# A new opening for a one-core encoder layer: products of ones while x lands, x in four transfers, a first power ahead of time, h by two engines, and two z heads ended before the other two

## The chip, the cores and the metric

The kernel runs on one core of one Trainium2 chip. Its engines work side by side, each in the order of its own queue: TensorE (PE, with its weight loads shown as PEld), VectorE (DVE), ScalarE (ACT), GpSimd (POOL) and SyncE (SP), which here issues every transfer between HBM and the on-chip memory. The metric is the device time of one execution in microseconds (us).

## The reference

One layer of a hybrid encoder runs over two sequences: a prompt of 2048 tokens and a sample of 32 tokens with a carried state. The width is 1024, everything is float32. What matters here:

```
cs = silu(c);  mod = cs @ ada_w + ada_b            # 6 x 1024 columns: shift, scale, gate, twice
h  = rmsnorm(x, norm_mix_g) * (1 + sc1) + sh1
p  = h @ w_in                                       # u, v | q, k, v | z | a, b
a_out = u * (W_s rmsnorm(v) + b_s)                  # spatial gating, 128-token chunks
q, k, v = silu(causal_conv(qkv));  q, k = l2norm(q), l2norm(k)
o  = gated_delta_rule(q, k, v, beta, g, state)      # 4 heads x 128, in chunks
b_out = rmsnorm(o) * silu(z)                        # z: 4 heads x 128 columns of p
x  = x + gt1 * (concat(a_out, b_out) @ w_out)
x  = x + gt2 * (relu((rmsnorm(x) * (1 + sc2) + sh2) @ w_up)^2 @ w_down)
y  = rmsnorm(x, final_norm_g)
```

The mean of squares in `rmsnorm` is taken over the 1024 features of a token. The features lie on the partitions (8 tiles of 128, counted by k), so that mean is a sum over partitions and tiles.

## The kernel before

The tokens are worked on in two halves (hf 0: tokens 0 to 1023, hf 1: the rest and the sample), and each half in groups of up to 512. Every large product is made three times with rounded operands: a matrix is split into a high part and the rest (`wh`, `wl` for weights, `BH`, `BL` for h; numbered 0 to 7 by k), and wh*BH, wh*BL and wl*BH are added up in PSUM. The splitting is one copy on ACT (the high part) and one subtraction on DVE (the rest). Weights come as slabs of 256 columns; a slab is loaded in two transfers, the first half of it for k 0 to 3, the second for k 4 to 7. Two slabs fit on the chip, so that the next one is split only when the last product of the one before it in the same place is done.

PSUM has eight banks, named by their use: g0, g1, g2 and L3 for the large products, C4 and C5, B6, M7. On-chip places are "slots" (s0 to s27). Most helpers record an operation: `act`, `tt` (two tensors), `ts` (tensor with scalars), `dma`, `mms` (products), `tr` (transpose on PE). All operations of one helper have one line in the profile: L339 for ACT, L354 for `tt`, L368 for `ts`, L377 for a DVE copy, L392 for the transfers, L400 for products, L411 for transposes.

The order is not that of the text. `Program.schedule` puts all recorded operations in an order by estimated costs and latencies, by a priority for each (the large products are behind everything else) and by the order in which they were recorded; each engine then runs its share of that order strictly. A change at the start thus moves work on every engine until the plan has settled again.

The opening, `startup`, does this for the first 512 tokens: load x (eight transfers of 128x512), square it on ACT, add the squares on DVE into `row`, then `rms_row`: four products with a column of ones (M7) give the sums per token, DVE scales them, POOL raises them to the power -0.5 (`rcol`), four transposes spread them over 128 partitions (M7), and ACT copies that to `row`. In parallel `ada_first(f, ps)` makes shift and scale for tile f: two transfers of 128x1024 (`ada0`, a ring of four places), two groups of four narrow products (C4 or C5; 2x256), an ACT copy, two transposes back, four small additions on DVE (`modc`) and one `ts` (the column `a1`). `h_tile` then multiplies x by `row` (DVE, for k 2 and 5 POOL), scales and shifts it (DVE, POOL or ACT by k) and splits it into `BH` and `BL`. For each k all four z heads get their three products (`gemm_k`; banks g0, g1, g2, L3; slab 0 serves heads 0 and 1, slab 1 heads 2 and 3). Then follow the second 512 tokens in the same manner, and `v_stage`, whose products (128x260) read h as the weights of PE. The mixers, the output projection and the feed-forward part come after that, unchanged in their code.

## Time and profile before

| | us |
|---|---|
| median of 3 runs | 2353.92 |
| lowest, highest | 2351.38, 2355.38 |
| the profiled execution, its own time | 2350.23 |
| its span, from the first to the last instruction | 2348.5 |
| PE busy | 2299.2 |
| DVE busy | 1678.7 |
| ACT busy | 1226.9 |
| POOL busy | 598.8 |

The profiled execution is 3.69 us shorter than the median and 1.7 us longer than its span. PE is busy for 98% of the span. In a row of the timeline stand the start, the busy time, the engine, the line, the operation, what it writes and reads, the shape and the count, and in brackets how long the engine had been idle and what ended that. PE counts each product of plain float32 operands twice in the profile (four products are x8), those of the split operands once.

### The profile page before, as it was taken

How to read it: one execution, taken by the hardware profiler on the slowest of the kernel's cores; microseconds unless marked ns; L12 is line 12 of the kernel's file. 1: busy time of each engine (PE TensorE's matmuls, PEld its weight loads, DVE VectorE, ACT ScalarE, POOL GpSimd, SP SyncE). 2: the span in 40 equal slices, each digit the busy share in tenths (PEclk: the TensorE clock that was granted, in tenths of full speed). 3: DMA queues.
4: the chain of work that ended last, by engine and by line, in shares of the span. 5: the costliest groups of instructions: out<-in, count | busy, mean ns of one | idle time of the engine just before them, and what ended most of it. 6: DMA issues, size and time to landing. Idle time of an engine off the chain costs nothing. (4 is left out here: it accounts for less than half of the span.)

```text
span 2348.5 us, 45724 instructions
## 1 busy us (share of the span) xinstructions
PE 2299.2 (98%) x15882; PEld 2171.3 (92%) x15882; DVE 1678.7 (71%) x3675; ACT 1226.9 (52%) x2817; POOL 598.8 (25%) x827
## 2 busy tenths in 40 slices
PE   7999999999999999999999999999999999999998
PEld 4877878999999888999999989999999999999998
DVE  6556557666665656589999999877667786666775
ACT  4465657455565535376555646664433564334343
POOL 2235421312432322445444434210000050000001
PEclk9999999999999999999999999999999999999999
DMA  9698668465557778888777787998667797666771
GB/s 321 225 333 280 199 189 258 141 187 178 151 175 228 241 220 251 256 269 270 243 252 259 258 269 248 335 323 266 211 219 250 251 294 247 214 220 219 238 232 53
DMA packets 369263, 556.27 MB, mean 237 GB/s; under 512 B 71212, under 2 KB 191424, under 8 KB 369032
## 3 DMA queue, kind: packets, MB, share of 16 engines
q1 hardware_dynamic: 369032, 553.35, 72.8%
q8 instruction: 125, 2.05, 0.4%
q14 instruction: 106, 0.87, 0.1%
HBM read 398.92 MB, written 154.28 MB: 236 GB/s over the span
## 5 line engine op out<-in xcount | busy, mean ns | idle before, releaser
L339 ACT ACTIVATE s<-s 128x348 fp32r<-128x348 f32 (+13 forms) x1079 | 494.9, 482 | 365.3 <-DVE s L354 145.5
L400 PE MATMUL f<-s,wh 128*128 128x348 f32 (+1 forms) x2760 | 662.0, 322 | 6.7 <-DVE s L359 5.4
L400 PEld LDWEIGHTS f<-s,wh 128*128 128x128 f32 x2760 | 480.2, 189 | 10.2 <-DVE s L359 6.2
L354 DVE TENSOR_TENSOR s<-f,s 128x348 f32<-128x348 f32 (+1 forms) x696 | 348.9, 514 | 175.3 <-PE f L400 174.2
L400 PE MATMUL f<-s,wl 128*128 128x348 f32 (+1 forms) x1380 | 444.1, 322 | 0.3 <-DVE wl L354 0.3
L400 PE MATMUL g<-BH,wh 128*128 128x512 f32 (+2 forms) x1112 | 421.8, 379 | 0.7 <-DVE s L359 0.7
L400 PE MATMUL g<-BH,wl 128*128 128x512 f32 (+2 forms) x1112 | 391.7, 352 | 0.0
L354 DVE TENSOR_TENSOR s<-s,s 128x348 fp32r<-128x348 f32 (+9 forms) x688 | 356.4, 547 | 49.2 <-ACT s L339 21.2
L400 PE MATMUL g<-BL,wh 128*128 128x512 f32 (+2 forms) x1112 | 390.6, 351 | 0.0
L400 PE MATMUL f<-BL,wh 128*128 128x348 f32 (+1 forms) x1016 | 329.0, 324 | 4.9 <-DVE BL L354 4.9
L400 PE MATMUL f<-BH,wl 128*128 128x348 f32 (+1 forms) x1016 | 328.1, 323 | 1.1 <-DVE wl L354 1.1
L400 PE MATMUL f<-BH,wh 128*128 128x348 f32 (+1 forms) x1016 | 328.4, 323 | 0.0
L339 ACT ACTIVATE wh<-s 128x512 fp32r<-128x512 f32 (+1 forms) x278 | 174.4, 634 | 240.1 <-PE f L400 180.9
L354 POOL TENSOR_TENSOR s<-s 64x39 f32<-64x39 f32 (+12 forms) x299 | 156.3, 523 | 433.9 <-issue 380.8
L400 PEld LDWEIGHTS f<-s,wl 128*128 128x128 f32 x1380 | 260.2, 189 | 0.6 <-DVE wl L354 0.6
L354 POOL TENSOR_TENSOR s<-s,s 128x512 f32<-128x512 f32 (+5 forms) x154 | 190.9, 1249 | 270.7 <-ACT s L339 118.4
L354 DVE TENSOR_TENSOR wl<-s,wh 128x512 fp32r<-128x512 f32 (+1 forms) x278 | 221.1, 803 | 20.4 <-ACT wh L339 20.0
L400 PEld LDWEIGHTS g<-BH,wh 128*128 128x128 f32 x1112 | 210.3, 189 | 23.8 <-issue 7.4
L400 PEld LDWEIGHTS g<-BH,wl 128*128 128x128 f32 x1112 | 209.2, 188 | 19.2
L400 PEld LDWEIGHTS g<-BL,wh 128*128 128x128 f32 x1112 | 210.6, 189 | 14.4 <-DVE BL L354 0.2
L359 DVE SCALAR_TENSOR_TENSOR s<-s,s,s 128x256 f32<-128x256 f32 (+5 forms) x318 | 161.9, 526 | 63.9 <-ACT s L339 39.6
L400 PEld LDWEIGHTS f<-BL,wh 128*128 128x128 f32 x1016 | 192.3, 189 | 6.5 <-DVE BL L354 6.5
(115 smaller groups left out, 3363.2 us busy)
## 6 DMA issues: line engine op xcount, KB each, us to landing
s<-w_u SPq DMA_DIRECT2D x124, 256.0 KB, 3.8
s<-w_d SPq DMA_DIRECT2D x118, 256.0 KB, 3.1
wh<-su_d SPq DMA_DIRECT2D x113, 256.0 KB, 3.6
wl<-su_d SPq DMA_DIRECT2D x113, 256.0 KB, 3.9
wh<-sd_d SPq DMA_DIRECT2D x108, 256.0 KB, 3.1
wl<-sd_d SPq DMA_DIRECT2D x108, 256.0 KB, 3.7
wr<-w_b SPq DMA_DIRECT2D x42, 512.0 KB, 5.0
s<-adaw SPq DMA_DIRECT2D x32, 512.0 KB, 5.9
```

The source lines that it names most:

```text
L339: self.p.op(ACT, c, lambda: nc.scalar.activation(out=R(out), in_=R(in_), func=func, **{k: R(v) for k, v in kw.items()}), [out, accum], [in ...
L354: self.p.op(eng, c, lambda: e.tensor_tensor(out=R(out), in0=R(a), in1=R(b), op=op), [out], [a, b])
L359: self.p.op(DVE, c, lambda: nc.vector.scalar_tensor_tensor(out=R(out), in0=R(a), scalar=R(s), in1=R(b), op0=op0, op1=op1), [out], [a, s, b])
L400: nc.tensor.matmul(R(out), R(l), R(r), **kw)
```

## The change

Seven things change, all in `startup` and what it calls; the arithmetic stays the same.

- x of the first 512 tokens comes in four transfers of two tiles each instead of eight, and so does x of the second 512. The load of the sample's state s0 was the first transfer of all; it is now bound (`after=self.begun`) to the products of the z heads and is issued later.
- `stir` records products on PE whose result is never read: eight of 128x128 ones with ones at the start, and two with a part of x whenever a pair of tiles has landed.
- POOL takes one power of ones before anything else needs a power.
- `rms_row` no longer copies its row to on-chip memory in the first group; DVE multiplies x by the bank M7 itself. All eight tiles are multiplied on DVE and scaled and shifted on ACT; POOL has no part of it any more.
- The two transposes of `ada_first` become two products with `sel` (128x2), a matrix of four unit columns added up, which brings the four partial sums together; one addition into `modc` is left of four. Three small additions make `sel`.
- The ring of places for `ada0` has seven places instead of four, and the slabs of the opening have a third place for raw data (slot 20).
- The z heads are recorded in another order: for k 0 to 2 all four heads, then k 3 to 7 for heads 0 and 1, then k 3 to 7 for heads 2 and 3. Added dependencies (`after`) hold the narrow products, the first multiplications and two weight splits to that order.

On PE the queue up to the first large product was this (M7 takes the sums of squares, s0 to s3 and s25 to s27 hold `ada0`, s8 to s11 hold x, s24 is `row`):

```order
L400 MATMUL M7_498<-ones_92,s24_493 128x1 x4
L400 MATMUL C4_503<-s0_469,s17_486 2x256 x4
L400 MATMUL C4_503<-s1_470,s17_486 2x256 x4
L411 MATMUL M7_560<-ident_91,rcol0_94 128x128 x4
L411 MATMUL C4_503<-ident_91,s13_482 128x128 x2
L400 MATMUL C5_504<-s2_471,s17_486 2x256 x4
L400 MATMUL C5_504<-s3_472,s17_486 2x256 x4
L411 MATMUL C5_504<-ident_91,s13_482 128x128 x2
L400 MATMUL C4_503<-s0_469,s17_486 2x256 x4
L400 MATMUL C4_503<-s1_470,s17_486 2x256 x4
L400 MATMUL g0_505<-BH0_71,wh_499 128x512
L400 MATMUL g0_505<-BL0_79,wh_499 128x512
```

and is now this (ahead of it stand only the eight products of ones and three pairs like the first row, one for each earlier pair of x tiles):

```order
L401 MATMUL M7_556<-s11_481,ones_92 128x128 x2
L401 MATMUL C4_501<-s0_470,s17_487 2x256 x4
L401 MATMUL M7_564<-ones_92,s24_494 128x1 x4
L401 MATMUL C4_501<-s1_471,s17_487 2x256 x4
L401 MATMUL C4_501<-sel_93,s13_483 128x2 x2
L412 MATMUL M7_588<-ident_91,rcol0_95 128x128 x4
L401 MATMUL C5_502<-s2_472,s17_487 2x256 x4
L401 MATMUL C5_502<-s3_473,s17_487 2x256 x4
L401 MATMUL g0_507<-BH0_71,wh_503 128x512
L401 MATMUL g0_507<-BL0_79,wh_503 128x512
```

The unread products stand first, the product with `sel` has moved ahead of the transposes of M7, and one tile's narrow products fewer (two groups of C4) come before the first large product. On DVE the same stretch, from the scaling of the sums to the first `BL`, read before:

```order
L368 TENSOR_SCALAR rcol0_94<-M7_498 128x4
L354 TENSOR_TENSOR wl_500<-wr0_96,wh_499 128x1024
L354 TENSOR_TENSOR modc_87<-C4_503,s13_482 128x2x2
L354 TENSOR_TENSOR s8_477<-s8_477,s24_493 128x512
L354 TENSOR_TENSOR modc_87<-C4_503,modc_87 128x2x2 x3
L368 TENSOR_SCALAR a1_89<-modc_87,nrm_88 128x2
L368 TENSOR_SCALAR s8_477<-s8_477,a1_89,modc_87 128x512
L354 TENSOR_TENSOR modc_87<-C5_504,s13_482 128x2x2
L354 TENSOR_TENSOR s8_477<-s8_477,s24_493 128x512
L354 TENSOR_TENSOR modc_87<-C5_504,modc_87 128x2x2
L354 TENSOR_TENSOR s9_478<-s9_478,s24_493 128x512
L354 TENSOR_TENSOR BL0_79<-s8_477,BH0_71 128x512
```

and reads now:

```order
L369 TENSOR_SCALAR rcol0_95<-M7_564 128x4
L355 TENSOR_TENSOR modc_87<-C4_501,s13_483 128x2x2
L369 TENSOR_SCALAR a1_89<-modc_87,nrm_88 128x2
L355 TENSOR_TENSOR s8_478<-s8_478,M7_588 128x512 x2
L355 TENSOR_TENSOR wl_504<-wr0_97,wh_503 128x1024
L355 TENSOR_TENSOR BL0_79<-s8_478,BH0_71 128x512
```

The subtraction for the slab (`wl`) has moved behind the first two multiplications, which now read M7, and one `modc` is left of four. Further on, PE fills its time with projections while the small inversions of the delta rule (B6, 32x16) become ready. In the half of tokens 0 to 1023 the first of them stood here:

```order
L400 MATMUL g1_3135<-BH0_71,wh_2805 128x512
L400 MATMUL g1_3135<-BL0_79,wh_2805 128x512
L400 MATMUL g1_3135<-BH0_71,wl_2806 128x512
L400 MATMUL B6_2229<-s9_478,s24_493 32x16 x32
L400 MATMUL g1_3135<-BH1_72,wh_2805 128x512
```

and stands here now:

```order
L401 MATMUL g0_3195<-BH0_71,wh_2996 128x512
L401 MATMUL g0_3195<-BL0_79,wh_2996 128x512
L401 MATMUL g0_3195<-BH0_71,wl_2997 128x512
L401 MATMUL B6_2333<-s9_479,s24_494 32x16 x32
L401 MATMUL g0_3195<-BH1_72,wh_2996 128x512
```

Counted in large products from the start of the program, it has moved from behind the 1107th to behind the 1155th; the other seven groups of this form in that half have moved back by 45 to 63 as well. From about the 4430th of PE's 11906 rows on the order is the same as before.

The diff; left out are the arguments `after` that `tt`, `dma` and `mms` pass on.

```diff
@@ slab
-    def slab(self, src, n):
+    def slab(self, src, n, after=()):
...
-            self.tt(wl[:, s], raw, wh[:, s].f32(), ALU.subtract)
+            self.tt(wl[:, s], raw, wh[:, s].f32(), ALU.subtract, after=() if e else after)
@@ setup
+        self.sel = sb("sel", [P, 2])
...
-        rg("ada", [(s, 0) for s in range(4)], (P, 1024))
+        rg("ada", [(s, 0) for s in (0, 1, 2, 3, 25, 26, 27)], (P, 1024))
@@ startup
-        load = lambda g: [c(x[g][k], self.x_src(0)(k, 512 * g, 512)) for k in range(KT)]
-        row = [self.row[:, 512 * g : 512 * g + 512] for g in range(2)]
+        both = [[self.slot(s, 0, (P, 2, HALF))[:, :, :512] for s in xr[g]] for g in range(2)]
+        load = lambda g: [c(both[g][e], i["xT"][2 * e : 2 * e + 2, :, 512 * g : 512 * g + 512].rearrange("k p t -> p k t"),
+                            8 * P * 512) for e in range(4)]
+        row = self.row[:, :512]
...
+                if k % 2:
+                    self.stir(x[0][k][:, :P], 2)
+            return self.rms_row([row], 512, None)
 
+        self.stir(self.ones, 8)
+        self.tt(self.rcol[0], self.ones[:, :4], self.mhalf, ALU.pow, POOL)
         load(0)
...
+        self.tt(self.sel, self.ident[:, 0:2], self.ident[:, 32:34], ALU.add)
+        for e in (64, 96):
+            self.tt(self.sel, self.sel, self.ident[:, e : e + 2], ALU.add)
+        r = stats()
...
+        self.ada_first(0, ps[0])
+        num = lambda: (len(self.p.ops) - 1,)
+
+        def h(k, after=()):
+            t = x[0][k]
+            self.tt(t, t, r, ALU.mult, after=after)
+            mark = num()
+            self.act(t, t, AF.Identity, scale=self.a1[:, k, 0:1], bias=self.modc[:, 0, k, 0:1])
+            self.split(self.BH[k][:, :512], self.BL[k][:, :512], t)
+            return mark, num()
+
+        scaled = num()
+        low = [h(0)]
+        self.sq = self.slab_list()
+        self.raws += [self.slot(20, 0, (P, SLABW // 2))]
+        self.sn = self.slab(*self.sq.pop(0), low[0][0])
+        z = [self.sn, self.slab(*self.sq.pop(0), low[0][1])]
+        self.sn = z[1]
         zs = [self.bank(t) for t in "gggL"]
+        done = []
         for k in range(KT):
-            self.ada_first(k, ps[k % 2])
-            self.h_tile(0, 0, k, x[0][k], row[0], self.a1, 0)
-            for h in range(H):
-                self.gemm_k(zs[h][:, :512], *z[h // 2], h % 2, 0, 0, k)
+            if k:
+                self.ada_first(k, ps[k % 2], done[min(LATE - 1, k - 4) if k > 4 else k - 3] if k > 2 else ())
+                low.append(h(k, low[k - 2][1] if k > 1 else scaled))
+            for e in range(H if k < LATE else 0):
+                self.gemm_k(zs[e][:, :512], *z[e // 2], e % 2, 0, 0, k)
+            done.append(num())
+        for e in range(0, H, 2):
+            for k in range(LATE, KT):
+                for u in (e, e + 1):
+                    self.gemm_k(zs[u][:, :512], *z[u // 2], u % 2, 0, 0, k)
+        self.begun = done[-1]
...
+    def stir(self, x, n):
+        ps = self.bank("M")
+        self.mms([(ps[:, :P], self.ones, x, dict(start=True, stop=True))] * n, 250 * n)
@@ ada_first
-        for e in range(2):
-            self.tr(ps[:, 256 + 128 * e : 384 + 128 * e], ar[:, 128 * e : 128 * e + 128], self.ident)
+        self.mms([(ps[:, 256 + 2 * e : 258 + 2 * e], ar[:, 128 * e : 128 * e + 128], self.sel, dict(start=True, stop=True))
+                  for e in range(2)], 460)
         m = self.modc[:, 0:2, f]
-        for s in range(4):
-            part = ps[:, 256:512].re("p (e s r) -> p e s r", e=2, s=4)[:, :, s, 0:2]
-            self.tt(m, part, self.adab[:, 0:2, f] if s == 0 else m, ALU.add)
+        self.tt(m, ps[:, 256:260].re("p (e r) -> p e r", e=2), self.adab[:, 0:2, f], ALU.add)
@@ delta_chain
-                self.dma(S, self.i["s0"][h])
+                self.dma(S, self.i["s0"][h], after=self.begun)
```

40 lines of the change are left out of this document (20 added, 20 removed).

## The prediction

> **What bounds the kernel now.** I read the page first, then the stretches of the span, and then the timeline of the opening engine by engine. The page and the stretches:
>
> ```profile
> PE 2299.2 (98%) x15882; PEld 2171.3 (92%) x15882; DVE 1678.7 (71%) x3675; ACT 1226.9 (52%) x2817; POOL 598.8 (25%) x827
> ```
> ```profile
> 0.00:23.58 23.58, 8.57 (x65) 4.12 (x65) 12.85 (x28) 10.53 (x16) 5.98 (x13) 1.00 0.88 302
> 23.58:58.00 34.42, 33.82 (x200) 21.35 (x197) 22.15 (x56) 17.61 (x30) 7.88 (x11) 0.95 0.97 338
> 58.00:1000.00 942.00, 933.49 (x7351) 830.51 (x7350) 569.98 (x1568) 508.94 (x1342) 294.35 (x580) 1.00 0.70 219
> ```
>
> After a stretch's length come the busy times of PE, PEld, DVE, ACT and POOL, the granted clock, the share of the transfer engines and GB/s. Up to 23.58 us PE idles for 15.0 us. From there to 58 us, the z products of the first 512 tokens, it is idle for 0.6 us, though the transfers are nearly saturated too (0.97); to 1000 us it is idle for 8.5 us of 942. So the opening is worth what comes off the arrival of PE's first large product, less what is added to PE's queue behind it. The two edges of that stretch, and its clock:
>
> ```profile
> 12.71 1.87 PE L400 MATMUL M<-ones,s 128*128 128x1 f32 x8 [12.71 <-DVE s L354]
> 14.51 1.89 PE L400 MATMUL C<-s,s 128*2 128x256 f32 x16
> 16.85 1.11 PE L411 MATMUL M<-ident,rcol 128*128 128x128 f32 x4 [0.45 <-POOL rcol L354]
> ...
> 21.08 0.61 PE L400 MATMUL C<-s,s 128*2 128x256 f32 x8
> 23.03 0.61 PE L400 MATMUL C<-s,s 128*2 128x256 f32 x8 [1.34 <-DMA s<-ada]
> 23.58 0.66 PE L400 MATMUL g<-BH,wh 128*128 128x512 f32 x1
> 24.03 0.72 PE L400 MATMUL g<-BL,wh 128*128 128x512 f32 x1
> ...
> 27.51 0.50 PE L400 MATMUL g<-BH,wh 128*128 128x512 f32 x1
> ...
> 54.89 0.39 PE L400 MATMUL g<-BL,wh 128*128 128x512 f32 x1
> 55.12 0.40 PE L400 MATMUL g<-BH,wl 128*128 128x512 f32 x1
> 55.66 1.02 PE L400 MATMUL M<-ones,s 128*128 128x1 f32 x8
> 56.55 0.47 PE L400 MATMUL g<-BH,wh 128*128 128x512 f32 x1
> ...
> 58.02 0.28 PE L400 MATMUL g<-wh,BH 128*128 128x260 f32 x1
> ...
> 60.15 0.65 PE L411 MATMUL M<-ident,rcol 128*128 128x128 f32 x4 [0.52 <-POOL rcol L354]
> ```
> ```profile
> 24.00:26.00 2.00, 2.00 (x7) 0.50 1.03 410
> ```
>
> At full clock one large product follows another by 0.23 us (54.89 to 55.12). From 24 to 26 us the clock is 0.50, and the first seven large products come much further apart.
>
> **The way to the first product.** Its chain before, on ACT, DVE and POOL:
>
> ```profile
> 4.38 0.63 ACT L339 ACTIVATE s<-s 128x512 f32<-128x512 f32 x1 [1.29 <-DMA s<-xT]
> 7.30 3.95 ACT L339 ACTIVATE s<-s 128x512 f32<-128x512 f32 x6 [1.46 <-DMA s<-xT]
> ```
> ```profile
> 11.97 0.69 DVE L354 TENSOR_TENSOR s<-s,s 128x512 f32<-128x512 f32 x1
> ...
> 14.69 1.23 DVE L354 TENSOR_TENSOR wl<-wr,wh 128x1024 fp32r<-128x1024 f32 x1
> ...
> 18.63 0.69 DVE L354 TENSOR_TENSOR s<-s,s 128x512 f32<-128x512 f32 x1
> ```
> ```profile
> 14.86 1.94 POOL L354 TENSOR_TENSOR rcol<-rcol,mhalf 128x4 f32<-128x4 f32 x1 [13.29 <-DVE rcol L368]
> ...
> 59.06 1.03 POOL L354 TENSOR_TENSOR rcol<-rcol,mhalf 128x4 f32<-128x4 f32 x1 [2.05 <-DMA z_d<-s]
> ```
> ```profile
> 18.00 0.60 ACT L339 ACTIVATE s<-M 128x512 f32<-128x512 f32 x1 [1.15 <-PE M L411]
> ...
> 32.82 0.81 ACT L339 ACTIVATE s<-s,modc,a 128x512 f32<-128x512 f32 x1 [1.83 <-DVE a L368]
> 33.54 0.36 ACT L339 ACTIVATE s<-C 128x256 f32<-128x256 f32 x1
> 33.80 0.62 ACT L339 ACTIVATE BH<-s 128x512 fp32r<-128x512 f32 x1
> ```
>
> *x in four transfers, s0 later.* The last sum of squares ends at 11.97 + 0.69 = 12.66. ACT's eight squares at 0.66 each (3.95 / 6) take 5.3 us; started at 4.38 without a gap they would end at 9.7 and the sum at 10.4. At the other end the transfers of `ada0` and the slab, now issued straight behind x, share the engines with it, and nothing is gained. I take 11.5, the middle, since the gap of 1.46 us in the middle goes only if the larger transfers land as early as the small ones did.
>
> *The early power, no copy, `sel` ahead.* From the sums to the first multiplication it was 18.63 - 12.66 = 5.97. The power falls from 1.94 to 1.03 and the copy with its hand-over (0.63) goes. But PE's queue now has `sel` ahead of the transposes, and `sel` waits for the second narrow group and ACT's copy of it. At the slow clock: sums 1.92, narrow group 0.95 (half of 1.89), copy 0.36 with 0.1 of hand-overs, `sel` 0.9 (its 0.5, found below, times 1.87 over 1.02), transposes 1.11, hand-over 0.05: 5.4. At full clock: 1.07, 0.54, 0.46, 0.5, 0.65, 0.05: 3.3. I take 4.6, nearer the slow end, as the row of 12.71 is the same work after an idle start. The first multiplication then starts at 11.5 + 4.6 = 16.1 (ends 13.7 and 18.1).
>
> *h by two engines.* DVE does two multiplications and one slab subtraction ahead of `BL`: 0.60 + 0.60 + 1.15 from start to start, then 0.69 and 0.05, together 3.1. ACT's way (0.69, 0.81, 0.62 and hand-overs, 2.2) lies beside that. PE's product with `BL` starts at 19.2, taken as 19.3 (ends 16.8 and 21.2), against 24.03: **-4.7** (-7.2 to -2.8). The work taken from POOL costs nothing: DVE loses three `modc` additions a tile for two multiplications in all, and ACT's 17.61 us of 34.4 leave room for six more rows of 0.81.
>
> **The stretch of the z products.** Its inserts are priced by these rows:
>
> ```profile
> 38.66 0.40 PE L400 MATMUL L<-BH,wl 128*128 128x512 f32 x1
> 39.52 0.61 PE L400 MATMUL C<-s,s 128*2 128x256 f32 x8 [0.46 <-DMA s<-ada]
> ...
> 40.62 0.40 PE L400 MATMUL g<-BH,wl 128*128 128x512 f32 x1
> 40.95 0.61 PE L400 MATMUL C<-s,s 128*2 128x256 f32 x8
> 41.49 0.51 PE L400 MATMUL g<-BH,wh 128*128 128x512 f32 x1
> ```
> ```profile
> 46.10 0.38 PE L411 MATMUL C<-ident,s 128*128 128x128 f32 x2
> 46.23 0.47 PE L400 MATMUL g<-BH,wh 128*128 128x512 f32 x1
> 46.55 0.39 PE L400 MATMUL g<-BL,wh 128*128 128x512 f32 x1
> ```
>
> *Narrow groups.* One costs 41.49 - 40.62 - 0.23 = 0.64. Twelve instead of ten stand behind the first product, five of them now next to another (0.54): **+0.8** (+0.6 to +1.3).
>
> *`sel` for transposes.* A pair of transposes costs 0.13 and 0.09 on the next product, 0.22. No row shows `sel`. Below it is bounded by that same 0.22; above by the products with a column of ones, which also load 128x128 float32 weights for next to no columns: 56.55 - 55.35 = 1.2 for four, 0.6 for two. I take 0.5, near the upper row because it is the same kind. Seven against six pairs: 3.5 - 1.3 = **+2.2** (+0.2 to +2.9). DVE's three saved additions are not on PE's path.
>
> *Seven places for `ada0`.* The wait 38.66 + 0.23 to 39.52 is 0.63: **-0.6** (-0.6 to 0). In the transfer queue a load of `eye16` now stands ahead of the last two halves of `ada0` and waits for a narrow product of k 5; work of k 2 to 5 covers it, and if that cover is gone the wait of 0.6 is back.
>
> *Heads 0 and 1 first.* Worth 0: at 58.02 the next stage starts without a wait already. The unread products lie in idle time: 0 as well, from 0 to the M7 sums' 0.85 at the two clocks (1.87 and 1.02), which the front has taken in.
>
> *Second group.* The sums at 55.66 move behind the first 128x260 products, which is neutral; the wait of 0.52 at 60.15 goes: **-0.5** (-0.5 to 0). x of that group is issued earlier but for its last pair, which stands behind a slab load waiting for DVE.
>
> *Clock.* Slow rows cost 27.51 - 24.03 less five products, a pair and a narrow group (1.15 + 0.22 + 0.64): 1.5. I take **0** (-1.5 to 0). PE was busy for 4.9 us from 12.71 to 17.96 and the narrow products of 21.08 ran at full speed, yet the clock stood at 0.50 from 24 on; the new queue is no denser between the sums and 19 us. The Trainium skill, "TensorE: Matmul & The Clock Gate", Part 1, says that activity sustained for about 3.4 us releases the clock and an idle window of that length gates it again. By its first half the unread products would have the z products start warm, which makes the sum 1.5 lower; its second half speaks against the change, as PE mostly waits between them, and the row of 24.00 agrees with that half; whether the first holds here, the trace before can't show.
>
> Sum: -4.7 + 0.8 + 2.2 - 0.6 - 0.5 = -2.8. The profiled execution's 2350.23 lies 3.69 under the median of 2353.92; the sum is made in its rows and gives 2347.4 there, and 2351.1 by the median, which I forecast as 2351. What can be told from no change is about 0.2%, 4.7 us.
>
> **The rivals.** *Everything at its good end*: x lands early, the clock stays up. Front -6.6, clock -1.5, the rest +1.9: -6.2, 2347.7. For it: 15 idle us at the front. Against: the saturated transfers.
>
> *The front doesn't move*: the new transfers compete with x, whose squares end where they did, and `sel` takes what the power gave. Front -2.8, rest +1.9: -0.9, 2353.0. For it: PE waited 1.34 us for `ada0` at 23.03.
>
> *Slower by the delta rule*: its small inversions stand some 48 large products (11 us) further back in PE's queue. PE's waits between 60 and 1000 us are small now:
>
> ```profile
> PE L L400 <- ACT s L339: 1.8, 3, 0.8
> PE L L411 <- DMA s<-kq_d: 1.2, 1, 1.2
> ```
>
> If the later chain has no projections left to cover it at a half's end, up to 11 us are lost there: -2.8 + 11 = +8.2, 2362. It decides from 2.8 on and shows from 7.5. Against it: with waits of at most 1.2 us, the queue has room.
>
> **How the numbers follow.** My forecast 0.45 (2348.9 to 2353.3, 2.2 to either side, about half the way to the ends of its front), the good end 0.22, the unmoved front 0.15, the delta rule 0.18, most of it below its price. Faster by over 0.2%, under 2349.2: the good end and a third of the first, 0.38. Slower, over 2358.6: most of the delta rule, 0.16 and a little for what moves with it, 0.19. The rest 0.43. The range goes from 2344.5, every term at its best end (-9.0, and a little), to 2361 near the third rival's price.
>
> **What would show it.** After: the first `BL` product at 17 to 21 us and the first 128x260 product at 53 to 56; `sel` pairs 0.4 to 0.6 apart from their neighbours; the power at about 1.0; clock 0.50 in the first 3 us of the z products; PE idle between 60 and 1000 us still about 8 us. It is wrong if `sel` costs no more than a transpose, if the clock stays full, or if PE waits more on B6 or L3.

## The result

The changed kernel takes 2360.29 us (median of 22 runs, 2351.57 to 2369.94), the kernel before 2353.08 us (22 runs, 2346.22 to 2356.31). The ratio is 1.0034, 95% interval 1.0026 to 1.0042: 7.2 us slower by the medians and 8 by the ratio. That is more than the 0.2% that the prediction counted as no change, and not the way of its forecast; the time itself lies at the slow end of its range. The profiled execution has a span of 2357.6 us against 2348.5.

The changed kernel's page, and the three stretches that the prediction read (to the first product of z, to the first 128x260 product, to 1000 us), with the same columns:

```profile
PE 2313.8 (98%) x15930; PEld 2181.2 (93%) x15930; DVE 1675.2 (71%) x3652; ACT 1232.9 (52%) x2824; POOL 597.7 (25%) x824
```
```profile
0.00:20.23 20.23, 16.17 (x81) 11.10 (x81) 9.72 (x23) 9.89 (x16) 3.10 (x12) 1.00 0.89 336
20.23:55.84 35.61, 35.58 (x221) 24.04 (x221) 19.18 (x37) 21.61 (x37) 4.28 (x7) 1.00 0.86 317
55.84:1000.00 944.16, 929.62 (x7296) 823.01 (x7295) 571.07 (x1563) 508.80 (x1340) 296.12 (x580) 0.99 0.70 218
```

The first stretch is 3.35 us shorter and the second holds no idle time. The third had 8.5 us of idle PE before; now it has 14.5, and the clock is no longer 1.00. The front in PE's timeline of the changed kernel (start, duration, operation, idle time ahead and its releaser):

```profile
12.66 1.84 PE L401 MATMUL M<-ones,s 128*128 128x1 f32 x8
14.43 1.03 PE L401 MATMUL C<-s,s 128*2 128x256 f32 x8
15.97 1.01 PE L401 MATMUL C<-sel,s 128*128 128x2 f32 x4 [0.50 <-ACT s L340]
16.84 1.09 PE L412 MATMUL M<-ident,rcol 128*128 128x128 f32 x4
...
21.05 0.80 PE L401 MATMUL g<-BL,wh 128*128 128x512 f32 x1
...
27.17 0.50 PE L401 MATMUL C<-sel,s 128*128 128x2 f32 x4
27.53 0.48 PE L401 MATMUL L<-BH,wh 128*128 128x512 f32 x1
...
55.84 0.28 PE L401 MATMUL g<-wh,BH 128*128 128x260 f32 x1
...
58.32 1.02 PE L401 MATMUL M<-ones,s 128*128 128x1 f32 x8 [0.52 <-DVE s L355]
```

The first 128x260 product stands at 55.84 against 58.02, but the second group's sums, which stood ahead of it (0.89 from 55.66 to 56.55), now come behind it. Like for like the opening is 1.3 us ahead. PE's waits behind it, from the same kernel's table of waits between 60 and 1000 us (line, releaser, total, times, longest):

```profile
PE B L401 <- issue: 3.2, 1, 3.2
PE M L401 <- DVE s L360: 2.8, 1, 2.8
PE M L401 <- POOL s L355: 1.9, 1, 1.9
PE M L412 <- POOL rcol L355: 1.6, 1, 1.6
```

The largest before was 1.2. The stretch from the first 128x260 product to the feed-forward's first (the v stage, the mixers and the output projection; "the mixers" from here on) is best compared by itself. Its row of before, and of the changed kernel (length, PE busy, clock, share of the transfer engines, GB/s):

```profile
58.02:1015.93 957.91, 949.40 (x7460) 1.00 0.70 220
```
```profile
55.84:1026.53 970.69, 956.15 (x7468) 0.99 0.70 218
```

12.8 us longer: 6.0 more of waits, and the rest of PE running at half clock, which follows the long waits. In rows of 1 us from the end of the wait of 2.76 us at 81.40, in the changed kernel:

```profile
81.40:82.40 1.00, 1.00 (x4) 0.50 0.06 25
82.40:83.40 1.00, 1.00 (x7) 0.50 0.23 66
83.40:84.40 1.00, 1.00 (x7) 0.52 0.90 230
84.40:85.40 1.00, 1.00 (x13) 1.00 0.85 207
```

Three waits (2.76, 1.90, 3.23) are followed so, the middle one for twice as long. Summed over rows of 5 us, (1 - clock) x length is 6.85 us in the changed kernel and 0 before. Length less waits less this is 949.3 and 949.4: PE's own work in the mixers changed by no more than the second group's sums (0.9), which the changed kernel's stretch holds besides, and waits and half clock are the loss. The feed-forward took 1331.07 us against 1332.57.

### The profile page after: what moved, and what is told of

Its sections match the earlier page's. It is cut to its first block, busy times and chain, and to the rows that moved or that the text cites. A ratio compares the mean times of both kernels' runs of the same rounds, so it can differ in the third digit from the quotient of the medians.

```text
span 2357.6 us, 45794 instructions
## 1 busy us (share of the span) xinstructions
PE 2313.8 (98%) x15930; PEld 2181.2 (93%) x15930; DVE 1675.2 (71%) x3652; ACT 1232.9 (52%) x2824; POOL 597.7 (25%) x824
## 3 DMA queue, kind: packets, MB, share of 16 engines
q8 instruction: 126, 2.06, 0.4%
## 5 line engine op out<-in xcount | busy, mean ns | idle before, releaser
L355 DVE TENSOR_TENSOR s<-s,s 128x348 fp32r<-128x348 f32 (+7 forms) x682 | 351.9, 545 | 54.5 <-ACT s L340 26.6
L355 POOL TENSOR_TENSOR s<-s,s 128x512 f32<-128x512 f32 (+4 forms) x152 | 189.5, 1254 | 281.6 <-ACT s L340 170.2
L360 DVE SCALAR_TENSOR_TENSOR s<-s,s,s 128x256 f32<-128x256 f32 (+4 forms) x318 | 163.9, 532 | 69.1 <-ACT s L340 40.4
L355 DVE TENSOR_TENSOR wl<-wr,wh 128x512 fp32r<-128x512 f32 (+2 forms) x160 | 153.3, 960 | 66.8 <-ACT wh L340 66.4
```

The source lines that it names most:

```text
L355: self.p.op(eng, c, lambda: e.tensor_tensor(out=R(out), in0=R(a), in1=R(b), op=op), [out], [a, b], after=after)
L360: self.p.op(DVE, c, lambda: nc.vector.scalar_tensor_tensor(out=R(out), in0=R(a), scalar=R(s), in1=R(b), op0=op0, op1=op1), [out], [a, s, b])
```

## The experiments

The table has both kernels and every run: where the first 128x260 product stands, the mixers' length, PE's waits in it (length less busy), the loss at half clock, and the median time with its ratio to the kernel before on the same chip. The chips differ by up to 2 us, so kernels of different rows are compared by the ratio. The columns of the trace come from one execution each, and executions of one kernel lie several us apart (the profiled one of the joined kernel is 5.5 us under its median, that of the last row 5.6 over it): they show where a wait is, and not each us of a median. In the rows named after the kernel before, and in the third row, the second group's sums stand ahead of the first 128x260 product, elsewhere behind it and so within the mixers.

| kernel | first 128x260 | mixers | waits | half clock | time | ratio (95%) |
|---|---|---|---|---|---|---|
| before | 58.02 | 957.9 | 8.5 | 0 | 2353.08 | |
| changed | 55.84 | 970.7 | 14.5 | 6.9 | 2360.29 | 1.0034 (1.0026-1.0042) |
| new opening, old order | 59.84 | 957.9 | 7.8 | 0 | 2352.86 | 1.0009 (0.9997-1.0020) |
| old opening, new order | 57.39 | 968.0 | 12.9 | 6.9 | 2359.32 | 1.0031 (1.0020-1.0042) |
| changed, three groups later | 56.18 | 967.9 | 13.5 | 1.7 | 2360.41 | 1.0034 (1.0021-1.0047) |
| before, 3400 ns | 62.81 | 961.1 | 12.1 | 0 | 2350.42 | 0.9989 (0.9980-0.9998) |
| joined | 53.45 | 963.7 | 10.5 | 3.4 | 2354.07 | 1.0013 (1.0004-1.0023) |
| joined, no ones | 57.77 | 969.3 | 14.8 | 5.1 | 2359.20 | 1.0035 (1.0023-1.0047) |
| joined, transposes | 54.75 | 965.8 | 12.8 | 1.7 | 2354.44 | 1.0010 (1.0001-1.0020) |
| changed, no ones | 56.38 | 963.2 | 10.3 | 3.4 | 2351.95 | 1.0005 (0.9994-1.0016) |
| changed, no ones, later | 56.14 | 967.7 | 12.8 | 0 | 2354.53 | 1.0010 (0.9999-1.0020) |
| joined, gate later | 57.20 | 970.2 | 13.9 | 5.1 | 2363.25 | 1.0040 (1.0026-1.0054) |
| before, 46 products | 65.06 | 966.7 | 15.1 | 1.8 | 2362.54 | 1.0041 (1.0027-1.0055) |
| before, 52 products | 68.67 | 965.0 | 12.5 | 3.4 | 2370.06 | 1.0076 (1.0062-1.0090) |
| changed, no ones, 3300 ns | 58.24 | 956.9 | 8.2 | 0 | 2346.64 | 0.9975 (0.9964-0.9985) |
| the same, 3400 ns | 57.95 | 963.9 | 11.1 | 1.7 | 2356.73 | 1.0017 (1.0005-1.0029) |
| the same, 3700 ns | 56.03 | 973.0 | 17.6 | 5.2 | 2364.73 | 1.0051 (1.0037-1.0064) |
| before, 3600 ns | 59.94 | 962.2 | 10.6 | 0 | 2353.88 | 1.0008 (0.9999-1.0017) |
| before, 3300 ns | 57.99 | 963.0 | 13.3 | 0 | 2355.75 | 1.0021 (1.0010-1.0031) |
| changed, 3300 ns | 58.86 | 964.9 | 13.5 | 0 | 2353.59 | 1.0004 (0.9995-1.0013) |

### The opening or the order behind it

The program is recorded twice, as changed and as before. Behind the opening both record the same operations in the same sequence, so the planner's start times of one can set the order of the other.

```diff
-            for o in self.p.schedule():
+            for o in self.pinned():
+        key = [o.start for o in ops[:n]] + [o.start + move for o in rest]
+        # emitted by the smallest key whose predecessors are out
```

> The changed opening, all of it, and behind it every instruction of every engine in the order of the kernel before: the list order is taken from a second recording of the old program. Nothing is left out. Theory A (the opening gains 1 to 3 us, and what it loses is lost by the new order of the later stages): 2350 to 2352, ratio 0.9985 to 0.9995, and the waits of TensorE on the gating product (2.8 us in the changed kernel), on the squares' sums (1.9) and on the reciprocals (1.6) are gone. Rival B (the opening itself puts x(1), the constants and the second slab late, and the later stages pay for that in any order): 2357 to 2361, ratio 1.002 to 1.0035.

> The old opening, and behind it every instruction of every engine in the order that the changed kernel has there. Nothing is left out. Theory A: slower than before by 6 to 11 us, ratio 1.0025 to 1.0047, with TensorE waiting 1.5 to 3 us at the gating product, at the squares' sums and at the reciprocals as in the changed kernel. Rival B: within 1.5 us of before, since the order by itself costs nothing.

The mixers' rows of the two, new opening with the old order first:

```profile
59.84:1017.75 957.91, 950.10 (x7461) 1.00 0.70 220
```
```profile
57.39:1025.41 968.02, 955.15 (x7467) 0.99 0.70 219
```

The old order takes 957.91 us behind either opening. The new order takes 968 behind the old opening, which makes that kernel as slow as the changed one. So the loss comes with the order of the mixers, and rival B is out; that the same order can also run without the loss is seen further down. The time of the first was over theory A's, because joining the two plans made ACT wait for the second group's x while z's products needed `BH`: PE waited 2.06 us at 47.73, and its first 128x260 product came 1.8 us late.

### The waits, one by one

The three groups that waited are set later in the queue (numbers count operations behind the opening):

```diff
+LATER = {**dict.fromkeys(range(236, 240), 3200), **dict.fromkeys(range(595, 598), 2000), **dict.fromkeys([655, 659, 660, 661], 2400)}
+        key = [o.start + LATER.get(j - n, 0) for j, o in enumerate(ops)]
```

> The changed kernel with three small groups of TensorE's products set later in its queue, by 3.2, 2.0 and 2.4 us of the planner's time: the first gating products of the second stage, and the reciprocals' transposes and the sums of squares of the third. Nothing is left out. Theory A1 (these three waits of 2.8, 1.6 and 1.9 us and the slow clock behind each are the loss): 5 to 8 us faster than the changed kernel, 2352 to 2355, ratio to before 1.0 to 1.001. Rival A2 (the order loses it in many small places, or what was waited for is then waited for elsewhere): 0 to 3 us faster than the changed kernel, ratio 1.002 to 1.0035.

Its largest waits in the timeline are these:

```profile
86.06 1.16 PE L410 MATMUL M<-s,s 128*128 128x128 f32 x8 [1.38 <-DVE s L364]
...
365.62 0.23 PE L410 MATMUL B<-s,s 32*32 32x16 f32 x1 [3.27 <-issue]
...
458.27 0.38 PE L421 MATMUL C<-ident,s 128*128 128x128 f32 x2 [1.74 <-DVE s L364]
```

The three waits went, and 5.1 us of half clock with them, but others of 1.38 and 1.74 took their place, the mixers were only 2.8 us shorter, and the time did not move: A2. (The profiled execution is 4.6 us under the median here.) PE's own work came out 3 us longer here (952.7); why stays open.

To keep the opening's lead, the second group's squares and h tiles are left in the changed opening's own order, and only the mixers are pinned to the old one (`n` is then the count at the end of `startup`).

> The changed opening in its own order up to the constants' loads, the second group's squares and h tiles among it, and from the mixers on every instruction in the order of the kernel before, so that no engine waits early for the second group's x as it did in the run with both sides pinned (first 128x260 product there at 59.84, before 58.02, changed kernel 55.84). Nothing is left out. Theory A (the opening is worth about 1.3 us once the sums that moved behind it are counted, and the old order costs the mixers 958 us from the first 128x260 product to the first of the feed-forward): first 128x260 product at 55.5 to 56.5, 958 to 960 us from there, time 2350.5 to 2352.5, ratio 0.999 to 0.9998. Rival B (the lead is eaten by the mixers in the old order too): ratio 1.0 to 1.001, with 960 us or more from the first 128x260 product.

The lead came, and larger than expected: the first 128x260 product stands at 53.45, behind three of them PE waits 0.89 us for the second group's sums, and the rest follows from 55.75. At the first gating products, which came at 78.94 without a wait before, it is gone:

```profile
80.74 0.87 PE L411 MATMUL M<-s,s 128*128 128x128 f32 x4 [3.66 <-DVE s L370]
```

They multiply what DVE makes from the second stage's v, and DVE has the second group's h in the same stretch. In no run with the changed opening did they start before 80.14. A PE that arrives earlier waits there, and after a long wait runs at half clock as well: rival B, with 963.7 us and a ratio a little over its 1.001. So in this order the opening's lead is waited away.

Two parts of the opening were undone on top of this. Without ones:

```diff
-                if k % 2:
-                    self.stir(x[0][k][:, :P], 2)
-        self.stir(self.ones, 8)
```

> As the run with the joined opening, without the products of ones; these feed nothing, so nothing of the result is left out. Theory A (the products of ones end before TensorE has work and the clock is slow from 20 to 26 us with them and without): first multiplication of the first h at 17.5 to 18.3 as with them, first 128x260 product within 0.7 us, same time. Rival B (they bring the full clock to the first products of z in some runs, as in the run with both sides pinned, where the first product took 0.49 us and not 0.80): without them the first 128x260 product comes 1.5 to 3 us later.

Transposes and four additions again in `ada_first`:

> As the run with the joined opening, with the eight narrow groups transposed by the identity and added by four additions, as before, in place of the products with the chosen columns. Nothing is left out. From the prediction's step (the products with the columns cost 0.22 us more for each group than the transposes' 0.22, of eight groups): TensorE's own time falls by 1 to 2 us between the first product of z and the first 128x260 product, while the modulation comes later by three additions of VectorE, so the first multiplication is unmoved and the first `BL` product comes 0 to 0.6 later. Total: within 1.5 us of the joined run, to the fast side. Rival (the four additions on VectorE hold up `BL`, and with it TensorE): 1 to 3 us slower.

Without ones the first 128x260 product came at 57.77, 4.3 us later, though the first product of z stood at 19.76 against 20.11. This is the clock: the large products ran at full speed from the first on in the joined kernel and at half until 31.4 us without ones. Rival B names that, but one execution each does not show that the ones did it, since with ones the full clock also came as late as 32.2 (last section). A stop at 798 us (below) and a wait of 4.52 us at the gate spoil the total. With transposes the first `BL` product stood at 23.41 against 20.94, 2.5 later and not 0 to 0.6, since they waited 2.37 us for ACT's copy of the second narrow group; the stretch from there to the first 128x260 product was 1.2 us shorter, though it began at half clock. In these two executions the products with `sel` are 1.3 us ahead at the first 128x260 product; the times, 2354.44 and 2354.07, show no difference.

Later groups once more, in the changed kernel without the ones (the three groups, and a fourth by 1500 ns), and in the joined kernel, where only the first gating products move:

```diff
+        for j in range(236, 240):
+            key[self.n0 + j] += 4000
```

> The changed kernel without the products of ones, and with the small groups later in TensorE's queue as in the run with three groups later (the second chunk's gating products 1.5 us later too). Nothing of the result is left out. Without the products of ones alone the mixers took 963.2 us from the first 128x260 product to the first of the feed-forward, with waits of 2.73 at the first gating product and 1.69 at the sums and two stretches of 3.4 us at half clock behind them. Theory (waits and the slow clock behind the long ones add up): the two waits and both stretches go, some 1.5 us come back as shorter waits elsewhere, so 957 to 960 us there and 2346 to 2350 in all, ratio 0.9975 to 0.9995. Rival (the loss is spread, and what one wait gives back the next one takes): 961 to 964 us there, ratio 1.0 to 1.001.

> The run with the joined opening and the old order of the mixers, with the first gating products 4 us later in TensorE's queue (they waited 3.66 us at 80.74 there, with 3.4 us at half clock behind), and six products of ones of two columns more at the start, which only move the place of the later instructions by 24, so that no pair of groups of 32x32 products takes up one whole block of 256 instructions. Nothing is left out. Theory: 961.4 falls to 956 to 958.5 us between the first 128x260 product and the feed-forward, and the time to 2346 to 2349.5, ratio 0.9975 to 0.999: the opening's lead of 2.3 us is kept only if nothing of TensorE waits for the second group's gate. Rival (the gate's late input holds later products too): 960 us or more, ratio 1.0 to 1.0015.

Both rivals held, and the mixers came out longer than either had it (967.7 and 970.2). The half clock went in the first (3.4 to 0), but the mixers became 4.5 us longer: waits of 0.8 to 1.7 us came elsewhere, one for a transfer of `adaw` at 175.67, and 5 us are in PE's own work, unexplained. In the second the gate no longer waited, but `adaw` (2.27), a reciprocal (1.40) and a stop without releaser (2.38) did.

### The stop without releaser

At 364 us of the changed kernel stand two groups of 64 small products, the second cut before its last:

```profile
362.63 0.73 PE L401 MATMUL B<-s,s 32*32 32x16 f32 x64
...
364.14 0.71 PE L401 MATMUL B<-s,s 32*32 32x16 f32 x63
368.08 0.18 PE L401 MATMUL B<-s,s 32*32 32x16 f32 x1 [3.23 <-issue]
```

The list of transfer queues on its page has two for instructions (packets, MB, share), and between 365 and 366 us one packet of the first starts:

```profile
q8 instruction: 126, 2.06, 0.4%
q14 instruction: 106, 0.87, 0.1%
```
```profile
q1 hardware_dynamic: 308, 0.37, 101.2%
q8 instruction: 1, 0.02, 5.8%
```

2.06 MB in 126 packets are 16 KB each. PE's weight loads, products and semaphore instructions are 32296 in this trace, 256 to each of the 126 packets, so a packet of this queue is a block of 256 instructions of 64 bytes for PE. In the compiled list of PE's instructions, the product that comes after the stop is number 4548, 17 x 256 + 196; in the trace, which lacks a few rows of that list, 4545 stand before it.

> The changed kernel without its five groups of products of ones, every other instruction in the same order; these products feed nothing, so nothing of the result is left out. It moves the place of every later product of TensorE in the list of instructions by the same number. In the changed kernel and in the run with three groups later TensorE stops for 3.2 us between the 63rd and the 64th of the same group of 32x32 products, at 368 and 365 us, with no releaser, while one packet of the queue of instructions lands. Theory F (it waits there for its instructions, and the place of the stop hangs on the number of instructions ahead): the stop of 3.2 us is gone or at another place, and with it about 1.5 us of slow clock, so 3 to 5 us faster than the changed kernel, 2355 to 2357, unless the opening gives some back. Rival D (the stop is a dependence of this group): the stop of 3.2 us stays at the 64th product of that group and the time is within 2 us of the changed kernel.

> The kernel before, with 46 products of ones of two columns at the start, which feed nothing and stand ahead of the first sums, for which TensorE waits until 12.7 us anyhow. They move the place of each later product in TensorE's list by 184 instructions of 64 bytes. Nothing is left out. Where the changed kernel stops at 368.08, the run with three groups later at 365.62 and the run with the joined opening without ones at 798.36, the instruction's number in the list leaves 195 to 197 over after division by 256 each time, and a whole block of 256 lies within two groups of 64 or 66 small products. By 184 no block of this kernel lies so. Theory F: no wait of 1.5 us or more without releaser, 957 to 959 us from the first 128x260 product to the feed-forward, time within 2 us of before. Rival D (no such rule): a stop or none, as it may come.

> The same with 52 of these products: 208 instructions. By the rule of the block of 256, two pairs of groups are now hit, the second (the 63rd of 64 products of its second group, near 344 us) and the fourth (the 59th of 64). Theory F: a stop of TensorE without releaser in one or both of them, of 1.5 to 3.5 us each, with 1.7 to 3.4 us of half clock's loss behind each stop over 1.8 us, so 3 to 9 us more than with 46 products, 2355 to 2361. Rival D: as with 46 products, within 1.5 us.

Without the ones the same group runs through (362.41, x64), and the changed kernel is as fast as before: 1.0005 against 1.0034, some 7 us, with the order of every engine the same in both traces but for the ones. Theory F holds, and rival D is out. It also means that the new order behind the new opening costs little where the ones are missing. The mixers lost 7.5 us: the stop and its half clock (3.2 + 1.7), half of the slow stretch behind the sums (1.7), 0.9 of other waits. That the total moved so much was more than theory F gave, and why is open. The two that followed can't be read by their times: the products of two columns took 0.215 us each half and put the sums from 12.7 to 20.9 and 23.5. By place they answer. With 52 the second pair stops at its 63rd product for 2.17 us, as named in advance:

```profile
358.64 0.71 PE L400 MATMUL B<-s,s 32*32 32x16 f32 x62
361.52 0.20 PE L400 MATMUL B<-s,s 32*32 32x16 f32 x2 [2.17 <-issue]
```

The fourth does not. With 46, where none was expected, there were two (1.30 and 1.65), behind the pair, at numbers 4548 and 7364. The rule had been drawn too narrowly: a block need not lie within the pair, it must only be used up too soon.

Eleven stops of 0.7 to 3.3 us near such pairs were seen, all at a number that leaves 196 by 256 (4548 five times, 7364, 10948, 12484, 13508 twice, and one 12 instructions behind the third pair in the kernel before with 3400 ns). Counted in the traces alone, all eleven leave 193 or 194, and behind 58 us no trace has another idle time of PE over 0.3 us without a releaser. PE went on some 3.5 to 6 us after the block ahead had begun. Of 18 blocks that PE used up in 3 us or less, the stop left out, eight ended in such a stop; of all that took longer, three (3.1 to 4.5 us). A block of 128 large products takes 29 us at 0.23 each. The last two were named by the number before they ran, with 3700 ns at the 59th of 64, and in the changed kernel with 3300 ns just behind the eighth pair:

```profile
366.71 0.68 PE L401 MATMUL B<-s,s 32*32 32x16 f32 x58
369.23 0.29 PE L401 MATMUL B<-s,s 32*32 32x16 f32 x6 [1.84 <-issue]
```
```profile
843.37 0.74 PE L401 MATMUL B<-s,s 32*32 32x16 f32 x66
845.36 0.49 PE L401 MATMUL g<-BH,wh 128*128 128x512 f32 x1 [1.25 <-issue]
```

> The same with 3700 ns. Here a block of 256 instructions begins 8 instructions behind the start of the second pair of groups of 32x32 products and ends 11 ahead of its end, at the 59th of 64 products of the second group. Theory F: TensorE stops there, between the 58th and the 60th product of that group, without releaser, for 1.5 to 3.5 us (the block before was under way for less than 2.5 us, and the six stops seen so far ended 4.1 to 5.7 us after the block's start). Against it: no stop there, as at some other pairs that were hit. Time by theory L 2350 to 2362.

With 3700 ns PE stopped where and about as long as named, though the time lies over the 2350 to 2362 of the text. So PE waits there for its next 16 KB of instructions, and 70 instructions more or less ahead decide whether it does. Not each such block stops, and what decides among the blocks used up fast is open. The Trainium skill, "Runtime: NRT & Kernel Launch", section "Instruction fetch mechanics", has the blocks of 256 and calls the cost of crossing one mostly hidden; these rows show up to 3.3 us, and more with the clock.

### Other draws of the planner

One constant, with no change in the work. Theory L, told in full in the fourth text, says that the mixers take PE's own work, its waits and the half clock behind long waits, and that the waits fall as the planned order happens to:

```diff
-DMA_LATENCY = 3500
+DMA_LATENCY = 3300
```

> The kernel before, with one number of its planner changed: a transfer is planned to take 3400 ns and not 3500 until it lands. No instruction is added, removed or changed, only their order. Nothing is left out. Theory A (the time hangs on what order the planner happens to find, by several us): 3 us or more away from before, to either side. Rival B (the order that the planner finds is about as good for any small change of its input): within 2 us of before, ratio 0.9992 to 1.0008.

> The kernel before with 3600 ns in the planner: same instructions, another order. Nothing of the result is left out. Theory L: 3 us or more from the kernel before, and rather slower, since the order of before has 8.5 us of waits in the mixers and no half clock, the least of all runs so far (the run with 3400 had 12.1): 2353 to 2360. Rival (a small change of the planner's input moves nothing): within 2 us.

> The kernel before with 3300 ns in the planner: same instructions, another order. Nothing of the result is left out. It tells what of the 5.75 us that the changed opening without ones won with 3300 ns (2346.64 against 2352.39) is the opening. If the 3300 ns alone make a good order: 2346 to 2349, as fast as the changed opening with the same number. If the opening is needed for it: 2350 to 2358. By theory L no single case can be foreseen, only that the mixers take 956 to 970 us.

> The changed kernel without the products of ones, and with the planner counting 3300 ns and not 3500 until a transfer lands: same instructions, another order. Nothing of the result is left out. Theory L (the mixers take 949.4 us of TensorE's own work plus its waits plus the half clock behind the long waits, and the waits come out of the planned order as it may fall, 8 to 20 us of them): 957 to 970 us from the first 128x260 product to the feed-forward, waits at other places than in the same kernel with 3500, time 2347 to 2360. Rival G (the changed opening makes the gate's input late, in every order): a wait of 1.5 us or more at the first gating products, near 80 us, as in five kernels with the changed opening before it.

> The same with 3400 ns. Theory L: as with 3300, and the three times of 3300, 3400 and 3500 lie 3 us or more apart. Rival G: a wait of 1.5 us or more at the first gating products, and the three times within 3 us. No block of 256 instructions lies within a pair of groups of small products here, so no stop without releaser of over 1.5 us inside a group is expected.

> The changed kernel, products of ones and all, with 3300 ns in the planner. Nothing is left out. Its order is that of the run with 3300 ns without the ones, which took 2346.64, plus the five groups of ones; their 70 instructions move a block of 256 so that it ends one instruction behind the eighth pair of groups of small products. Theory L and F: 956 to 959 us for the mixers where the eighth pair does not stop, and 1.3 to 3.5 us more, with 1.7 of half clock, where it does, near 850 us: 2344 to 2351, ratio 0.997 to 0.9995. Against it: over 2353, the changed opening as it was made is slower in any order.

The kernel before stayed within 0.21% with three other constants (2350.42, 2353.88, 2355.75); for the first two theory A and theory L had forecast 3 us or more, and that did not hold. The changed opening without ones drew 2346.64, 2356.73, 2351.95 and 2364.73 with 3300, 3400, 3500 and 3700 ns, 18 us apart, as theory L has it, though the first and the last lie outside the ranges that it gave. Rival G failed with 3300 and 3400 ns, where z's products ended later (58.24 and 57.95) and PE found the gate's input ready:

```profile
81.06 1.15 PE L401 MATMUL M<-s,s 128*128 128x128 f32 x8
```

The later end need not be the order's doing: the first product of z stood at 20 us as in the others, but the large products ran at half speed until 32 and 31 us, where with 3700 ns, which did wait at the gate, they did until 27. The row is that of the run with 3300 ns, the fastest of all, with 0.9975 (0.9964 to 0.9985), 5.75 us better than before and 13.7 better than the changed kernel. Its mixers are the shortest, with few waits and no half clock:

```profile
58.24:1015.16 956.92, 948.75 (x7468) 1.00 0.71 221
```

It is not the opening's lead that wins: the first 128x260 product stands at 58.24. Nor is it the constant alone, since the old opening with 3300 ns took 2355.75. Its profiled execution, 2350.6 us, is the slowest of its eight and no faster than the profiled one of before (2350.23), so the trace does not show where the gain is. With the ones put back it took 2353.59, over the 2344 to 2351 of its text and on the side that the text counts against the changed opening; the stop at 845 us is 1.25 of these 7 us, other waits about 4 in the trace, and why they came is open.

## Why the prediction was wrong

*The last sum of squares at 11.5* was one miss: the four transfers landed 1.36 us apart, the squares began at 5.78 and not 4.38, and the sum ended at 12.51, at the slow end of its range. Rows of ACT and of DVE in the changed kernel:

```profile
5.78 1.15 ACT L340 ACTIVATE s<-s 128x512 f32<-128x512 f32 x2 [3.07 <-DMA s<-xT]
...
9.87 1.15 ACT L340 ACTIVATE s<-s 128x512 f32<-128x512 f32 x2 [0.20 <-DMA s<-xT]
```
```profile
11.82 0.69 DVE L355 TENSOR_TENSOR s<-s,s 128x512 f32<-128x512 f32 x1
...
17.97 1.29 DVE L355 TENSOR_TENSOR s<-s,M 128x512 f32<-128x512 f32 x2 [0.46 <-PE M L412]
```

*From the sums to the first multiplication* took 17.97 - 12.51 = 5.5, where 4.6 was taken of 3.3 to 5.4. The terms at the slow clock were near, all of them (1.84, 1.03, 1.01, 1.09, against 1.92, 0.95, 0.9, 1.11); the choice toward the middle was wrong. The power was right, and so was the rest of the way:

```profile
14.86 1.02 POOL L355 TENSOR_TENSOR rcol<-rcol,mhalf 128x4 f32<-128x4 f32 x1 [12.20 <-DMA s<-w_b]
```

From the multiplication to `BL`'s product it took 3.08 where 3.1 stood. The front gave -2.98 and not -4.7, inside its range.

*Behind it*, narrow groups, `sel` and the `ada0` wait summed to +2.4; the stretch without the second group's sums grew from 33.10 to 34.79, +1.7. A warm `sel` pair took 0.36 (27.17 to 27.53), not 0.5. The `ada0` wait went. The 0.5 us at the second group's reciprocals came to nothing, since its sums now wait 0.52. *The clock* taken at 0 was right for these two executions: large products ran 0.6 apart until 26 us, and before until 27.

So the opening was worth -1.3 and not -2.8. But the sign turned on a step that the sum left out. It has no term for the new order of the stages behind 58 us; "PE idle between 60 and 1000 us still about 8 us" was one of its signs, and the order stood only in the third rival, against which it said "with waits of at most 1.2 us, the queue has room". In its place the runs show that the re-planned order costs 0.31% behind the old opening, where no stop for instructions occurs. In the changed kernel it costs 12.8 us of mixers: waits of 1.6 to 2.8 us at small products (gate, sums, reciprocals) that PE's fixed order reaches before DVE or POOL have their input, one of 3.2 for instructions, and 6.9 us at half clock. It does not cost this at every arrival: with the ones left out, the same order came to 1.0005. So the ones, priced at 0, are a second term that the sum lacks: in this order they cost some 7 us, of which the trace shows 4.9 as the stop for instructions and the half clock behind it, while the joined kernel was 5 us slower without them. The third rival's time of 2362 was near by luck, since its mechanism was not what happened: no wait at the delta rule's inversions for want of projections was seen, though the stop for instructions fell into one of their groups.

Heads 0 and 1 first, priced 0, was not run alone and stays open, and so do the seven places.

## What to carry to other kernels

Where a planner fixes every engine's order ahead of time, a change in one stage can draw the order of the later stages anew; pin the later order to tell the change from the draw, before judging either, and then try a few draws. Price a wait of a small product on a busy PE by its length and by the half clock behind it, and ask of each lead gained at the front at which input of another engine it will be waited away. Don't read a us of an opening from one execution each, since the clock's turn alone moved its end by up to 5 us here. Count the instructions ahead of dense groups of small products, since their place in the list alone can cost some us.

## What had not been expected of the hardware

*The clock falls after waits of under 2 us.* Of 39 waits of PE of 1.3 us or more in the mixers of all traces, none of the 15 up to 1.65 us was followed by half clock, two of the six between 1.67 and 1.74 were, and all but one of the 18 from 1.79 us up. The length of the wait does not decide alone: in the feed-forward six of the eight waits of 1.3 to 1.65 us that met the full clock lost it, and four of the mixers' 23 stretches at half clock came behind waits of 0.5 to 1.2 us among small products. A stretch lasts 3.4 us (a loss of 1.7), in four cases 6.8 (3.4). The Trainium skill, "TensorE: Matmul & The Clock Gate", Part 1, has two states with half the clock in the one, and a free-running window of about 3.4 us; the stretches of 3.4 us agree with the window. It asks for a whole idle window before the clock falls; here 1.8 us were enough.

*The end of the opening goes with the moment at which the clock turns full.* With the changed opening the first product of z starts at about 20 us in nearly every run, but the large products reach full speed at 19.7 us in the joined kernel, 26.3 in the changed one, 28.1 without ones, 31.5 in the joined one without ones and 32.2 in the changed one with 3300 ns, and the first 128x260 product stands at 53.45, 55.84, 56.38, 57.77 and 58.86 in the same sequence. In four of the seven executions with ones the clock was full from some 5 to 6 us on, for 3.4 us, and fell back. It was full from 20 us through the z products in only two of the seven, and in none of the six without ones (27.4 to 32.2). So the ones can bring the warm start that the prediction left open, and mostly did not.

*The granted clock's column can miss a slow start.* In the changed kernel it says 1.00 from 0 on, while the large product at 21.05 took 0.80 us and those from 27 us 0.4 to 0.5; the trace's first record of the clock lies at 26.3 us. With the same opening in front of the old order, the column says 0.50 from 10 to 19 us and the same product takes 0.50.

*Narrow products don't warm PE.* The 104 halves of 52 products with two columns took 22.34 us, 0.215 each. The products with `sel`, of two columns too, give the scale: in the joined kernel without ones four halves took 0.85 us at half clock and 0.50 at full. So 22 us of them without a gap did not bring the full clock.
